# Level products of the chunked attention cut to their diagonal blocks and put in column groups of the array

## Chip, core and metric

The program runs on one core of one Trainium2 chip. The metric is the device time of one execution in microseconds, the median of three runs. TensorE (PE) has a matmul side and a weight-load side (PEld), VectorE is DVE, ScalarE is ACT, GpSimd is POOL, and SyncE (SP) issues nearly all transfers.

## What is computed

A two-layer trunk on 1024 latent and 128 context tokens of width 1024: a gated linear attention (GLA) layer, then a Fourier layer, each followed by a gated channel mixer. The change touches the GLA layer alone. For each of four heads (128 key channels, 256 value channels) and each of two scan directions:

```python
bcum = jnp.cumsum(gi, axis=2)
diff = bcum[:, :, :, None, :] - bcum[:, :, None, :, :]
decay = jnp.exp(jnp.where(lower[:, :, None], diff, -jnp.inf))
attn = jnp.einsum('bhik,bhjk,bhijk->bhij', qi, ki, decay)
o = (jnp.einsum('bhij,bhjv->bhiv', attn, vi)
     + jnp.einsum('bhik,bhkv->bhiv', qi * jnp.exp(bcum), state))
```

The weight of token j for token i has a decay that depends on the channel, so `attn` is no plain product of q and k.

## The kernel before

The kernel takes chunks of 128 tokens (nine of them: eight latent, one context), three to a column group `cg`, and does both directions at once. Within a chunk it builds the 128x128 matrix `A` (tile name `A`, keys on partitions, queries along columns) by levels. For a half block of s tokens in `LEVELS = (64, 32, 16, 8, 4, 2, 1)`, all pairs that lie in one block of 2s tokens but in different halves share a reference point, the boundary of the halves. The decay then splits into a factor on k and a factor on q: `e[:, 0]` and `e[:, 1]` (tile `le`) are made by a subtraction on POOL (line 535) and on DVE (537), one exponential on ACT (540), and a multiplication by k on POOL (541) and by q on DVE (546). The product of the two is taken for the whole 128x128 chunk, three chunks into one PSUM tile `lv` (line 549), and `copy_predicated` on DVE (551) takes from it, by a mask per level, what belongs to that level:

```python
for c in range(3):
    PE.matmul(ps[:, c * P:(c + 1) * P], lhsT=view(kk, kb + c * P, [1, P]),
              rhs=e[:, 1, c * P:(c + 1) * P], start=True, stop=True)
ins = V.copy_predicated(att.rearrange("p (c i) -> p c i", i=P), ...
```

The diagonal itself comes from an undecayed product of k and q (line 527), copied by ACT with a factor of 2 (528). So each cg has eight products of three matmuls, and there are twelve cg (four heads by three). All are fp32, and each fp32 matmul stands in the trace as two matmul records and two weight loads, here called passes. `A`, the states `sf` and `sb` and the values then make the output `o` (565 to 570), which is normed by way of `ov` (577) and multiplied by the gate `r`.

What surrounds it on PE: attention of head h is interleaved with the projections of head h+1 (`pr`, `pk`, `pq`, `pv`, lines 97 to 99, a product of three fp32r matmuls each), and head 3, which has no head after it, with its own `pr` and then with the first half of the output projection (`wo`). `mod_background` (line 175, tile `mods`) is a third strand: small products of 32 weight columns in four column groups of the array, given out by `tick` after every second level. The order on each engine is not written out by hand: the framework's scheduler lists the instructions by priority (`later(n)` moves a part back in it) as it simulates them, and each engine then runs its list in order. `le` has 4 buffers (tag `m3`, shared with `qb`), the PSUM tag of `lv`, `o`, `kt` and `kv` has 4, weight tiles `wr` have 2 and `wh` 6. The 14 buffers of tag `u` hold the normed input `Hp`, which the last `pr` product of head 3 reads; behind it they take the attention outputs `ot` that are read back, and the residual `x`.

Of the kernel before, what the change touches and what calls it, by code (L numbers as in the profile page):

```python
# [15 lines left out]
F32 = mybir.dt.float32  # L16
F32R = mybir.dt.float32r
I32 = mybir.dt.int32
U8 = mybir.dt.uint8
# [5 lines left out]
P = 128  # L25
# [5 lines left out]
CH = 384  # L31
# [14 lines left out]
def trunk(tc, a, o):  # L46
# [12 lines left out]
    def t15(name, dt=F32):  # L59
        return sb.tile([P, CH], dt, tag="t", bufs=5, name=name)  # L60

    def t30(name, dt=F32):
        return sb.tile([P, 2, CH], dt, tag="m3", bufs=4, name=name)
# [4 lines left out]
    def at_ps(name):  # L68
        return pp.tile([P, 512], F32, tag="at", bufs=4, name=name)
# [32 lines left out]
    def const(name, shape, dt=F32, src=None):  # L102
        t = con.tile(shape, dt, name=name)
        if src is not None:
            nc.sync.dma_start(t, src)
        return t
# [86 lines left out]
    def tick(n=1, behind=None):  # L193

        for _ in range(n):
            while queue:
                try:
                    with tc.issue_after(behind.ins) if behind else ExitStack():
                        next(queue[0])
                    break  # L200
                except StopIteration:
                    queue.pop(0)
# [177 lines left out]
    gng = const("gng", [P, 2], src=a["gng"])  # L380
    convw = const("convw", [P, 2, 3, NF], src=a["convw"])
    convb = const("convb", [P, 2, NF], src=a["convb"])
    mask = const("mask", [P, len(LEVELS), P], U8)
    mraw = sb.tile([P, 1032], F32, tag="wr", bufs=2, name="mraw")
    nc.sync.dma_start(mraw[:, :len(LEVELS) * P], a["mask"])
    V.tensor_copy(mask.rearrange("p l i -> p (l i)"), mraw[:, :len(LEVELS) * P])
    for ch in range(NCH):
        ev_glr(ch, pss[ch])

# [66 lines left out]
    def view(t, off, *dims):  # L456
        return bass.AP(tensor=t.tensor, offset=t.offset + off, ap=[list(t.ap[0]), *[list(d) for d in dims]])
# [21 lines left out]
    def kv(kt, v, c):  # L479
# [2 lines left out]
                  start=True, stop=True)  # L482
        return ps

    def attention(h, qk, pages):

        dec = sb.tile([P, 2, 9], F32, tag="dec", bufs=2, name="dec")
        for cg in range(3):
            S.activation(dec[:, :, 3 * cg:3 * cg + 3], view(pages[cg][:, BB], P - 1, [CH - P + 1, 2], [P, 3]),
                         AF.Exp, scale=1.0 / TAU)  # L490
        sf = page(f"sf{h}")
        nc.sync.dma_start(sf[:, :256], a["state"][0, h])
        for cg in range(3):
            v, bb = pages[cg][:, VV], pages[cg][:, BB]
            kt = khat(qk, bb, 0, cg)
            for c in range(3 * cg, 3 * cg + 3):
                if c == 7:
                    continue
                ps = kv(kt, v, c)
                if c == 8:  # L500
                    new_state(0, h, ps)
                else:
                    V.scalar_tensor_tensor(sf[:, (c + 1) * 256:(c + 2) * 256], sf[:, c * 256:(c + 1) * 256],
                                           dec[:, 0, c:c + 1], ps[:, :256], op0=ALU.mult, op1=ALU.add)
        yield
        s_b = sb.tile([P, 256], F32, tag="sb", bufs=4, name="sb")
        nc.sync.dma_start(s_b, a["state"][1, h])
        sbs = {7: s_b}
        for cg in (2, 1, 0):
            v, bb, r = pages[cg][:, VV], pages[cg][:, BB], pages[cg][:, RR]  # L510
            kt = khat(qk, bb, 1, cg)
            for c in range(3 * cg + 2, 3 * cg - 1, -1):
                if c == 0:
                    continue
                ps = kv(kt, v, c)
                if c == 8:
                    new_state(1, h, ps)
                else:
                    s_n = sb.tile([P, 256], F32, tag="sb", bufs=4, name="sb")
                    V.scalar_tensor_tensor(s_n, sbs[c], dec[:, 1, c:c + 1], ps[:, :256], op0=ALU.mult, op1=ALU.add)  # L520
                    sbs[c - 1] = s_n

            att = t15("A")
            ps = at_ps("lv")
            for c in range(3):
                s = cg * CH + c * P
                PE.matmul(ps[:, c * P:(c + 1) * P], lhsT=qk[:, s:s + P], rhs=qk[:, T + s:T + s + P], start=True, stop=True)
            S.activation(att, ps[:, :CH], AF.Copy, scale=2.0)
            for li, s in enumerate(LEVELS):
                nb = CH // (2 * s)  # L530
                base = cg * CH
                e = t30("le")
                ref = view(bb, s - 1, [2 * s, nb], [CH + 1, 2], [0, s])
                if s > 1:
                    G.tensor_tensor(view(e, 0, [2 * s, nb], [s, 2], [1, s]), ref,  # L535
                                    view(bb, 0, [2 * s, nb], [CH + s, 2], [1, s]), op=ALU.subtract)
                V.tensor_tensor(view(e, CH + s, [2 * s, nb], [-s, 2], [1, s]),
                                view(bb, s, [2 * s, nb], [CH - s, 2], [1, s]), ref, op=ALU.subtract)
                if s > 1:
                    S.activation(e, e, AF.Exp, scale=1.0 / TAU)  # L540
                    G.tensor_tensor(e[:, 0], e[:, 0], qk[:, base:base + CH], op=ALU.mult)  # L541
                    kk, kb = e, 0
                else:
                    S.activation(e[:, 1], e[:, 1], AF.Exp, scale=1.0 / TAU)
                    kk, kb = qk, base
                V.tensor_tensor(e[:, 1], e[:, 1], qk[:, T + base:T + base + CH], op=ALU.mult)
                ps = at_ps("lv")
                for c in range(3):
                    PE.matmul(ps[:, c * P:(c + 1) * P], lhsT=view(kk, kb + c * P, [1, P]),  # L549
                              rhs=e[:, 1, c * P:(c + 1) * P], start=True, stop=True)  # L550
                ins = V.copy_predicated(att.rearrange("p (c i) -> p c i", i=P),
                                  mask[:, li, None, :].to_broadcast([P, 3, P]),
                                  ps[:, :CH].rearrange("p (c i) -> p c i", i=P))
                if li % 2 == 0:
                    tick(1, behind=ins)
            qb = t30("qb")
            S.activation(qb, bb.rearrange("p (z i) -> p z i", z=2), AF.Exp, scale=1.0 / TAU)
            V.tensor_tensor(qb, qb, view(qk, T + cg * CH, [0, 2], [1, CH]), op=ALU.mult)

            po = [at_ps(f"o{d}") for d in range(2)]  # L560
            for d in range(2):
                for c in range(3):
                    cc = 3 * cg + c
                    out = po[d][:, c * P:(c + 1) * P]
                    PE.matmul(out, lhsT=v[:, c * 256 + d * P:c * 256 + (d + 1) * P], rhs=att[:, c * P:(c + 1) * P],
                              start=True, stop=(cc == 8))
                    if cc < 8:
                        PE.matmul(out, lhsT=sf[:, cc * 256 + d * P:cc * 256 + (d + 1) * P],
                                  rhs=qb[:, 0, c * P:(c + 1) * P], start=False, stop=False)
                        PE.matmul(out, lhsT=sbs[cc][:, d * P:(d + 1) * P],  # L570
                                  rhs=qb[:, 1, c * P:(c + 1) * P], start=False, stop=True)
            sq0, sq1 = t15("os0"), t15("os1")
            S.activation(sq0, po[0][:, :CH], AF.Square)
            S.activation(sq1, po[1][:, :CH], AF.Square)
            V.tensor_tensor(sq0, sq0, sq1, op=ALU.add)
            ps = at_ps("ov")
            PE.matmul(ps[:, :CH], lhsT=ones, rhs=sq0, start=True, stop=True)
            S.activation(sq1, ps[:, :CH], AF.Ln, bias=epsc[:, 0:1], scale=1.0 / 256.0)
            S.activation(sq1, sq1, AF.Exp, scale=-0.5)
            for d in range(2):  # L580
                o1 = t15("o1")
                V.scalar_tensor_tensor(o1, po[d][:, :CH], gng[:, d:d + 1], sq1, op0=ALU.mult, op1=ALU.mult)
                rv = r[:, d * CH:(d + 1) * CH]
                if h < 3:
                    V.tensor_tensor(rv, o1, rv, op=ALU.mult)
                else:
                    V.tensor_tensor(o1, o1, rv, op=ALU.mult)
                    split_ot(3, d, cg, o1)
            if h < 3:
                nc.sync.dma_start(ot_dram[h][:, :, cols(cg)].rearrange("d p t -> p d t"),  # L590
                                  r.rearrange("p (d t) -> p d t", d=2))
            yield
# [965 lines left out]
```

## Time and profile before

| what | value |
|---|---|
| median of 3 runs (lowest to highest) | 2561.12 us (2558.16 to 2563.42) |
| the profiled execution: time, span | 2564.86 us, 2563.0 us |
| PE, PEld busy in the span | 95%, 91% |
| DVE, ACT, POOL busy | 72%, 43%, 29% |
| mean granted TensorE clock | 0.981 of 2.4 GHz |
| mean DMA traffic | 121 GB/s |

Busy time of PE counts a matmul from its start to its modelled end, and matmuls overlap, so PE can look full while it moves little. Distances from start to start of matmuls say more. GLA attention lies between about 80 and 680 us. The profiled execution is 3.7 us above the median of the runs.

### The profile page before, as it was taken

Reading aid. Unit: us, or ns where it says so; the run is one execution under the profiler, and the core shown is the slowest. Engines: PE = TensorE matmul, PEld = TensorE weight load, DVE = VectorE, ACT = ScalarE, POOL = GpSimd, SP = SyncE. Lnnn points to the kernel's source line nnn. Section 1 sums busy time; section 2 is a strip of 40 time slices with the busy share of each in tenths; the row PEclk is TensorE's granted clock in tenths of the full one; section 3 lists DMA queues with packets and bytes.
Section 4 is the critical chain, followed back from the end, with each engine's and each line's share of the span. In section 5 each row is a group of like instructions: output and inputs, shape, how many; then the busy total and the mean of one; then the engine's idle time right before and its main releaser. Section 6 shows DMA issues by size and latency. Waiting matters only on the chain. (4 is left out here: it accounts for less than half of the span.)

```text
span 2563.0 us, 46543 instructions
## 1 busy us (share of the span) xinstructions
PE 2425.1 (95%) x18122; PEld 2329.2 (91%) x18122; DVE 1841.2 (72%) x3339; ACT 1089.3 (43%) x2086; POOL 730.9 (29%) x548
## 2 busy tenths in 40 slices
PE   5999999987999999999999998999899999999997
PEld 4998988877999999999999996998899999999997
DVE  7647475566699677777787877277987778778676
ACT  5435344445364323333345564344533333334553
POOL 3435454453202333444100005230144444410000
PEclk8999999998999999999999999999999999999999
DMA  7212222204233453232674357344223232267334
GB/s 263 69 54 89 80 80 82 67 21 146 87 116 124 132 172 104 91 96 83 212 248 135 112 153 216 107 156 144 90 87 117 83 96 87 80 229 224 93 86 125
DMA packets 200972, 309.85 MB, mean 121 GB/s; under 512 B 18288, under 2 KB 142064, under 8 KB 200752
## 3 DMA queue, kind: packets, MB, share of 16 engines
q1 hardware_dynamic: 196528, 302.66, 37.2%
q10 hardware_dynamic: 4224, 4.23, 0.5%
q8 instruction: 142, 2.33, 0.4%
q14 instruction: 78, 0.64, 0.1%
HBM read 233.71 MB, written 73.11 MB: 120 GB/s over the span
## 5 line engine op out<-in xcount | busy, mean ns | idle before, releaser
L98 PE MATMUL pd<-hl,wd 128*128 128x288 f32 x1112 | 328.7, 299 | 5.4 <-DVE hl L1085 5.2
L99 PE MATMUL pd<-hh,wd 128*128 128x288 f32 x1112 | 326.7, 297 | 0.0
L97 PE MATMUL pd<-hh,wd 128*128 128x288 f32 x1112 | 316.5, 298 | 5.5 <-ACT hh L1084 3.2
L809 POOL TENSOR_TENSOR s<-wa,s 128x512 fp32r<-128x512 f32 x114 | 157.0, 1377 | 278.6 <-ACT s L808 278.6
L1084 ACT ACTIVATE hh<-hr 128x288 fp32r<-128x288 f32 x308 | 133.2, 437 | 222.1 <-PE pd L98 213.3
L98 PEld LDWEIGHTS pd<-hl,wd 128*128 128x128 f32 x1112 | 210.8, 190 | 7.9 <-DVE hl L1085 7.4
L1085 DVE TENSOR_TENSOR hl<-hr,hh 128x288 fp32r<-128x288 f32 x308 | 138.5, 455 | 109.3 <-ACT hh L1084 108.7
L97 PEld LDWEIGHTS pd<-hh,wd 128*128 128x128 f32 x1112 | 204.2, 188 | 10.8 <-ACT hh L1084 5.7
L99 PEld LDWEIGHTS pd<-hh,wd 128*128 128x128 f32 x1112 | 210.4, 190 | 0.0
L809 POOL TENSOR_TENSOR a<-wa,a 128x512 fp32r<-128x512 f32 x76 | 100.1, 1318 | 334.7 <-ACT a L808 231.1
L808 ACT ACTIVATE s<-wa 128x512 fp32r<-128x512 f32 x120 | 75.5, 630 | 189.8 <-DVE wa L826 116.1
L977 ACT ACTIVATE hid<-hid 128x576 f32<-128x576 f32 x88 | 60.4, 686 | 161.5 <-DVE hid L972 102.0
L1074 DVE TENSOR_TENSOR wd<-wd,wd 128x512 fp32r<-128x512 f32 (+1 forms) x184 | 116.4, 642 | 9.7 <-ACT wd L1073 4.9
L808 ACT ACTIVATE a<-wa 128x512 fp32r<-128x512 f32 x80 | 50.3, 631 | 141.0 <-PE pa L99 76.2
L1073 ACT ACTIVATE wd<-wd 128x512 fp32r<-128x512 f32 (+1 forms) x184 | 104.4, 580 | 11.7 <-PE ps L99 4.0
L860 DVE TENSOR_TENSOR q<-q,ps 128x288 f32<-128x288 f32 x232 | 98.4, 444 | 10.1 <-PE ps L99 8.4
L535 POOL TENSOR_TENSOR le<-vbr 128x384 f32<-128x384 f32 x72 | 74.0, 1032 | 109.3 <-PE lv L549 95.5
L1208 POOL TENSOR_TENSOR fn<-fn 128x512 f32<-128x512 f32 x8 | 14.1, 1764 | 312.9 <-ACT wp L728 293.3
L541 POOL TENSOR_TENSOR le<-le,qk 128x384 f32<-128x384 f32 x72 | 91.6, 1278 | 35.6 <-ACT le L540 34.7
L97 PE MATMUL pa<-fh1x,a 128*128 128x288 f32 x320 | 95.3, 298 | 5.9 <-DVE c L860 3.6
L97 PE MATMUL ps<-fh1x,s 128*128 128x288 f32 x320 | 95.2, 298 | 3.0 <-DVE hid L917 3.0
L97 PE MATMUL ps<-fh0t,s 128*128 128x288 f32 x320 | 96.4, 302 | 1.4 <-DVE c L860 1.4
(689 smaller groups left out, 8852.5 us busy)
## 6 DMA issues: line engine op xcount, KB each, us to landing
hr<-hid SPq DMA_DIRECT2D x308, 144.0 KB, 2.2
wm<-in_wmod SPq DMA_DIRECT2D x112, 256.0 KB, 2.9
hid<-hid SPq DMA_DIRECT2D x44, 576.0 KB, 3.8
wa<-in_wup SPq DMA_DIRECT2D x40, 512.0 KB, 3.5
wg<-in_wup SPq DMA_DIRECT2D x40, 512.0 KB, 4.1
hid<-t SPq DMA_DIRECT2D x132, 144.0 KB, 3.3
wd<-in_wdn SPq DMA_DIRECT2D x16, 1024.0 KB, 8.0
wm<-in_wmod SPq DMA_DIRECT2D x96, 128.0 KB, 3.5
```

What stands on the lines that cost most here:

```text
L97: PE.matmul(ps, lhsT=wh, rhs=xh, start=first, stop=False, skip_group_check=skip)
L98: PE.matmul(ps, lhsT=wh, rhs=xl, start=False, stop=False, skip_group_check=skip)
L99: PE.matmul(ps, lhsT=wl, rhs=xh, start=False, stop=last, skip_group_check=skip)
L535: G.tensor_tensor(view(e, 0, [2 * s, nb], [s, 2], [1, s]), ref, view(bb, 0, [2 * s, nb], [CH + s, 2], [1, s]), op=ALU.subtract)
L541: G.tensor_tensor(e[:, 0], e[:, 0], qk[:, base:base + CH], op=ALU.mult)
L808: S.activation(w[name][:, :512], x, AF.Copy)
L809: (eng or G).tensor_tensor(w[name][:, 512:], x, w[name][:, :512].bitcast(F32), op=ALU.subtract)
L860: add.last = V.tensor_tensor(out[:, xs], x[:, xs], ps[s][:, :SUB], op=op)
L1073: S.activation(hi, x, AF.Copy)
L1074: low = V.tensor_tensor(lo, x, hi.bitcast(F32), op=ALU.subtract)
L1084: S.activation(hi[:, c], raw, AF.Copy)
L1085: V.tensor_tensor(lo[:, c], raw, hi[:, c].bitcast(F32), op=ALU.subtract)
```

## The change

Level s needs only the blocks of 2s tokens on the diagonal, so a product is now cut to them, but to no less than 32 columns: `n = max(2s, 32)`. The array is used in column groups: a matmul with `tile_position=(0, n*g)` takes n weight columns (keys) and n moving columns (queries), and writes to partitions n*g to n*g+n. The results of levels 16 to 1, and of the undecayed product, lie packed as 32 columns per chunk, in a new tile `near` of 96 columns; level 64 is unchanged on PE and is written to `A` first, by ACT, level 32 by a copy on ACT and one on DVE, and `near` is put into the four diagonal blocks of `A` at the end. The masks shrink to 32 columns. The files line up as 549 before, 492 after.

```diff
+    def diagonal(ps, n, kk, at, q):
+
+        for c in range(3):
+            for g in range(P // n):
+                PE.matmul(ps[n * g:n * g + n, c * n:(c + 1) * n], lhsT=view(kk, at + c * P + n * g, [1, n]),
+                          rhs=q[:, c * P + n * g:c * P + n * g + n], start=True, stop=True,
+                          **({} if n == P else dict(tile_position=(0, n * g))))
...
-    mask = const("mask", [P, len(LEVELS), P], U8)
+    mask = const("mask", [P, len(LEVELS) - 2, 32], U8)
...
-    V.tensor_copy(mask.rearrange("p l i -> p (l i)"), mraw[:, :len(LEVELS) * P])
+    for g in range(4):
+        b = slice(32 * g, 32 * g + 32)
+        V.tensor_copy(mask[b], mraw[b, 2 * P:len(LEVELS) * P].rearrange("p (l i) -> p l i", i=P)[:, :, b])
...
             ps = at_ps("lv")
-            for c in range(3):
-                s = cg * CH + c * P
-                PE.matmul(ps[:, c * P:(c + 1) * P], lhsT=qk[:, s:s + P], rhs=qk[:, T + s:T + s + P], start=True, stop=True)
-            S.activation(att, ps[:, :CH], AF.Copy, scale=2.0)
+            diagonal(ps, 32, qk, cg * CH, qk[:, T + cg * CH:T + (cg + 1) * CH])
+            S.activation(near, ps[:, :96], AF.Copy, scale=2.0)
...
-                for c in range(3):
-                    PE.matmul(ps[:, c * P:(c + 1) * P], lhsT=view(kk, kb + c * P, [1, P]),
-                              rhs=e[:, 1, c * P:(c + 1) * P], start=True, stop=True)
-                ins = V.copy_predicated(att.rearrange("p (c i) -> p c i", i=P),
-                                  mask[:, li, None, :].to_broadcast([P, 3, P]),
-                                  ps[:, :CH].rearrange("p (c i) -> p c i", i=P))
+                n = max(2 * s, 32)
+                diagonal(ps, n, kk, kb, e[:, 1])
+                if n == P:
+                    ins = S.activation(att, ps[:, :CH], AF.Copy)
+                elif n == 64:
+                    S.activation(att3[:64, :, :64], ps[:64, :192].rearrange("p (c i) -> p c i", i=64), AF.Copy)
+                    ins = V.tensor_copy(att3[64:, :, 64:], ps[64:, :192].rearrange("p (c i) -> p c i", i=64))
+                else:
+                    ins = V.copy_predicated(near.rearrange("p (c i) -> p c i", i=32),
+                                            mask[:, li - 2, None, :].to_broadcast([P, 3, 32]),
+                                            ps[:, :96].rearrange("p (c i) -> p c i", i=32))
...
+            for g in range(4):
+                b = slice(32 * g, 32 * g + 32)
+                src = near[b].rearrange("p (c i) -> p c i", i=32)
+                if g % 2:
+                    S.activation(att3[b, :, b], src, AF.Copy)
+                else:
+                    V.tensor_copy(att3[b, :, b], src)
```

A product so has 12 matmuls of 32 columns, or 6 of 64, where it had 3 of 128. As the scheduler sees other instructions, it also lays out another order of all engines through the whole of the GLA layer; behind it, from the Fourier layer's preparation on, the order is the same.

The first place is PE in head 0, its second cg (h=0, cg=1), where attention runs beside the `pv` projection of head 1. Before, from the undecayed product on:

```order
L527 MATMUL lv<-qk_686 128x128 x3
L549 MATMUL lv<-le 128x128 x4
L186 MATMUL mods_1554<-sel,mrow_1830 128x8
L549 MATMUL lv<-le 128x128 x5
L175 MATMUL mods_1856<-wm_1826,cs 32x128 x4
L175 MATMUL mods_1856<-wm_1828,cs 32x128 x4
L549 MATMUL lv<-le 128x128 x3
```

Now, in the same place:

```order
L492 MATMUL lv<-qk_689 32x32 x12
L492 MATMUL lv<-le 128x128 x3
L492 MATMUL lv<-le 64x64 x6
L492 MATMUL lv<-le 32x32 x9
L186 MATMUL mods_1580<-sel,mrow_1906 128x8
L492 MATMUL lv<-le 32x32 x15
L98 MATMUL pv_1793<-wv10l,h_303 128x256
L175 MATMUL mods_1945<-wm_1902,cs 32x128 x4
L175 MATMUL mods_1945<-wm_1904,cs 32x128 x4
L99 MATMUL pv_1793<-wv10h,h_303 128x256
L97 MATMUL pv_1793<-wv10h,h_304 128x256
```

The products still stand in blocks, but a stretch in column groups now starts and ends more often.

The second place is PE in head 3, its last cg (h=3, cg=0), where the only other work is the output projection `wo`. Before:

```order
L549 MATMUL lv<-le 128x128
L97 MATMUL wo_5503<-ot_5150,wo01h 128x384
L549 MATMUL lv<-le 128x128
L98 MATMUL wo_5503<-ot_5150,wo01h 128x384
L549 MATMUL lv<-le 128x128
L99 MATMUL wo_5503<-ot_5150,wo01l 128x384
```

Now:

```order
L492 MATMUL lv<-le 32x32
L98 MATMUL wo_6249<-ot_5720,wo03h 128x384
L492 MATMUL lv<-le 32x32
L99 MATMUL wo_6249<-ot_5720,wo03l 128x384
L492 MATMUL lv<-le 32x32
L97 MATMUL wo_6249<-ot_5723,wo03h 128x384
L492 MATMUL lv<-le 32x32
L98 MATMUL wo_6249<-ot_5723,wo03h 128x384
```

Before, single matmuls of a product alternated with `wo` too, three to a product, and both were of the full array; now it is twelve to a product in column groups, each between two full matmuls, and they have moved from `wo01` and `wo02` to the end of `wo02` and to `wo03`.

The third place is PE at the end of the same cg, where the last level is followed by `o` (588, 591, 593). Now:

```order
L492 MATMUL lv<-le,qk_4270 32x32
L99 MATMUL wo_6320<-ot_5723,wo03l 128x384
L492 MATMUL lv<-le,qk_4270 32x32 x9
L588 MATMUL o_6708<-A,vbr_5377 128x128
L591 MATMUL o_6708<-qb,sf_5652 128x128
L593 MATMUL o_6708<-qb,sb 128x128
```

Before, `o` of this cg alternated with `wo02`, and the whole of `wo03` (72 matmuls) stood behind it. Now all of the first half of `wo` stands in front, and behind the 18 matmuls of `o` come 18 of the second half that need no output of this cg. The cg before it (h=3, cg=1) changes in a similar way: its undecayed product alternates with `pr` one by one, and its other products stand in one block behind the last `pr`, where they alternated with `pr` before.

Counted over the whole program, PE goes from full matmuls into column groups and back 111 times before and 252 times now. 28 of the stretches are now a single `mods` product, of 2 before: in three places, beside `pr` of heads 0 to 2, eight of them that stood together alternate one by one with `pr`.

## Rows read from the trace of the kernel before

**Rows 1.** The page, busy time of the engines and the granted clock by 40 slices

```profile
PE 2425.1 (95%) x18122; PEld 2329.2 (91%) x18122; DVE 1841.2 (72%) x3339; ACT 1089.3 (43%) x2086; POOL 730.9 (29%) x548
...
PEclk8999999998999999999999999999999999999999
```

**Rows 2.** Stretches: us, busy PE, PEld, DVE, ACT, POOL; clock, DMA, GB/s

```profile
128.00:560.00 432.00, 407.26 (x3032) 371.39 (x3031) 253.34 (x403) 187.09 (x322) 196.64 (x153) 0.99 0.23 70
560.00:680.00 120.00, 102.08 (x599) 97.73 (x598) 74.87 (x116) 49.52 (x77) 43.02 (x29) 0.91 0.31 107
```

**Rows 3.** Waits, 80 to 660 us: in total, times, longest

```profile
POOL le L535 <- PE lv L549: 95.5, 46, 11.3
```

**Rows 4.** Tile lv: durations min/median/max in ns, first and last start

```profile
L549 PE MATMUL lv<-le x432: 270/275/378, 128.2 to 648.5; 128*128 128x128 f32 x144
L551 DVE COPY_PREDICATED A<-mask,lv x84: 572/584/608, 129.2 to 650.5; 128x384 f32<-128x384 uint8 x84
```

**Rows 5.** Order of time on PE, full, column, full: start, duration, passes

```profile
226.94 1.06 PE L549 MATMUL lv<-le 128*128 128x128 f32 x8
227.92 0.64 PE L175 MATMUL mods<-wm,cs 128*32 128x128 f32 x16
228.50 0.94 PE L549 MATMUL lv<-le 128*128 128x128 f32 x6
229.19 0.36 PE L97 MATMUL pv<-wv11h,h 128*128 128x256 f32 x1
```

**Rows 6.** Order of time on PE, column stretches between three fp32r matmuls

```profile
135.13 0.42 PE L175 MATMUL mods<-wm,cs 128*32 128x128 f32 x8
135.49 0.44 PE L99 MATMUL pr<-h,wr00l 128*128 128x384 f32 x1
135.77 0.34 PE L97 MATMUL pr<-h,wr00h 128*128 128x384 f32 x1
135.94 0.33 PE L98 MATMUL pr<-h,wr00h 128*128 128x384 f32 x1
136.21 0.43 PE L175 MATMUL mods<-wm,cs 128*32 128x128 f32 x8
```

**Rows 7.** Order of time on PE, a column stretch of two groups

```profile
1545.39 0.41 PE L175 MATMUL mods<-wm,cs 128*32 128x128 f32 x4
```

**Rows 8.** Between the cg of head 3: stretches, as rows 2

```profile
580.00:610.00 30.00, 16.15 (x96) 14.09 (x96) 22.99 (x37) 24.29 (x38) 12.39 (x10) 0.79 0.39 129
610.00:660.00 50.00, 49.61 (x301) 48.79 (x299) 27.51 (x46) 11.00 (x18) 13.57 (x9) 0.95 0.40 143
```

**Rows 9.** Order of time on PE there, in brackets what ended its wait

```profile
588.25 0.49 PE L565 MATMUL o<-A,vbr 128*128 128x128 f32 x2 [2.47 <-DVE A L551]
597.37 1.34 PE L577 MATMUL ov<-os,ones 128*128 128x384 f32 x2 [2.91 <-DVE os L575]
605.76 0.69 PE L97 MATMUL wo<-ot,wo00h 128*128 128x384 f32 x1 [7.05 <-ACT wo00h L86]
```

**Rows 10.** Tile le: durations min/median/max in ns

```profile
L535 POOL TENSOR_TENSOR le<-vbr x72: 826/916/1552, 81.5 to 640.2; 128x384 f32<-128x384 f32 x72
L540 ACT ACTIVATE le<-le x72: 827/844/850, 94.3 to 642.8; 128x768 f32<-128x768 f32 x72
L541 POOL TENSOR_TENSOR le<-le,qk x72: 1006/1316/1817, 98.5 to 643.8; 128x384 f32<-128x384 f32 x72
```

**Rows 11.** Order of time on ACT and PE after the last cg of head 3

```profile
658.48 0.47 ACT L574 ACTIVATE os<-o 128x384 f32<-128x384 f32 x1
661.57 0.89 PE L577 MATMUL ov<-os,ones 128*128 128x384 f32 x2 [1.96 <-DVE os L575]
665.35 0.95 ACT L601 ACTIVATE ot<-o 128x384 fp32r<-128x384 f32 x2
```

**Rows 12.** Stretches on PE: us, busy (instructions), granted clock, DMA, GB/s

```profile
1544.00:1548.00 4.00, 3.39 (x31) 1.00 0.99 328
...
1556.00:1560.00 4.00, 4.00 (x27) 0.60 0.95 278
```

More of the change, by code (lines that the diff above doesn't have):

```diff
@@ L523, in attention @@
             att = t15("A")
+            att3 = att.rearrange("p (c i) -> p c i", i=P)
+            near = sb.tile([P, 96], F32, tag="near", bufs=2, name="near")
             ps = at_ps("lv")
-            for c in range(3):
-                s = cg * CH + c * P
-                PE.matmul(ps[:, c * P:(c + 1) * P], lhsT=qk[:, s:s + P], rhs=qk[:, T + s:T + s + P], start=True, stop=True)
-            S.activation(att, ps[:, :CH], AF.Copy, scale=2.0)
+            diagonal(ps, 32, qk, cg * CH, qk[:, T + cg * CH:T + (cg + 1) * CH])
+            S.activation(near, ps[:, :96], AF.Copy, scale=2.0)
             for li, s in enumerate(LEVELS):
```

## The prediction

> **What bounds the kernel now.** I read the page first. PE is busy 95% of the span, at almost the full clock, and POOL only 29% [rows 1]. A mean over the program says little of one layer, so I cut the span into stretches next. In the attention of heads 0 to 2, PE is busy 407.26 of 432 us while DVE, ACT and POOL have much room [rows 2]. The waits agree: POOL, which begins each level, stands 95.5 us until PE has read a `le` buffer and frees it [rows 3]. So here PE sets the pace, and only PE time counts. The next look is at head 3, where PE loses 18 us in 120 [rows 2]: nearly 14 of them lie in 580 to 610, where it is busy 16.15 of 30, while the 50 us behind are packed, 49.61 busy [rows 8]. The single events name the cause: chains through `o` and `ov`, then weights `wo00h` that ACT rounds late [rows 9].
>
> **Prices on PE.** A product of three full fp32 matmuls is six passes; the trace has six from 228.50 to 229.19 [rows 5], so about 0.67 to 0.69 us a product at 0.112 a pass. The duration of one record, 0.275 [rows 4], is no price, since passes overlap.
>
> Twelve matmuls of 32 columns are 24 passes. If four column groups run at once, that is six rounds. The trace has such groups already, with 128 moving columns, in `mods`. Two runs of 8 passes start at 135.13 and at 136.21, with three fp32r matmuls of 384 between [rows 6]; such a matmul takes 0.17 when the next follows directly (135.77 to 135.94). So the run costs 1.08 - 3 x 0.17 = 0.57 us. Sixteen passes take 0.64 as recorded where eight take 0.42 [rows 5, 6], which is 0.22 for two rounds, 0.11 a round, what one full pass takes. Hence 0.57 = 2 x 0.11 + 0.35: about 0.34 us a run is the fixed price of going into column groups and back (PE empties, weights are loaded uncovered). Do groups run at once? A run of four passes (two groups) has 0.41, one of eight 0.42 or 0.43 [rows 6, 7]: yes.
>
> No row shows 32 moving columns. A round lies between a quarter of 0.11, 0.028, if it follows the columns, and 0.11, if it doesn't shrink. I take 0.028, since an fp32r matmul of 384 columns at 0.17 does follow its columns, and keep 0.11 as the other end. With it:
>
> - a block of 12 alone: 0.34 + 6 x 0.028 = 0.51, for 0.67
> - six of 64 columns alone: 0.34 + 6 x 0.055 = 0.67, no gain
> - a **single** 32-column matmul between two full ones: 0.34 + 2 x 0.028 = 0.40; twelve of these are 4.75 us, seven times what the product took
> - a change from 64 to 32 columns inside a stretch, estimated at 0.13 (one reload; bounds 0 to 0.34).
>
> So everything turns on how often PE changes modes, and this goes from 111 to 252.
>
> **The change part by part.**
>
> Heads 0 to 2, nine cg, products in blocks (the first place). Seven of eight products change, 7 x 0.67 = 4.7 us. Now: five more stretches, 1.7; six products of 32 columns, 36 rounds, 0.99; level 64's half blocks, 0.35; one reload 0.13: 3.17. That is -1.5 a cg, **-13.7** for nine. Against it, eight `mods` products that stood together alternate with `pr` in three places: seven or eight more stretches and their first rounds uncovered, 3.7 us each, **+11.1**; two further splits **+0.8**.
>
> Head 3, first cg (in blocks): **-1.9**. Second cg: twelve singles 4.75 and the rest in one block 2.36, against 8 x 0.67 = 5.4: **+1.7**. Last cg (the second place): 49 singles and a pair, 50 x 0.40 = 19.8; six single 64-column ones at 0.475, 2.85; blocks of 12 and 9, 1.0; the uncut product 0.67: 24.3 against 5.4, **+18.9**. It lies in the packed stretch [rows 8], so nothing covers it: POOL, ACT and POOL need 0.92, 0.84 and 1.32 for a level [rows 10], while PE now needs 12 x (0.40 + 0.17) = 6.8.
>
> The gap at 580 to 610. The last `pr` now stands ahead of the second cg's levels, and ACT and POOL round `wo00` ahead of that cg's `os`, so the 7.05 us wait [rows 9] should shrink. The last levels, which stood among `pr`, now stand behind it with nothing beside them; four `le` buffers cover all but about three levels, each 0.92 + 0.84 + 1.32 = 3.1 us from POOL to POOL, two of them overlapping: some 6 us of idle stay of 13.9. **-8**; bounds 0 and -13.9.
>
> The tail. From `os` at 658.48 through `ov` to `ot` ending at 666.3 is 7.8 us, with PE waiting 1.96 at `ov` [rows 11]; the rest was covered by `wo03`. Only 18 x 0.17 = 3.1 us of `wo` stand behind now: 7.8 - 3.1 - 1.96 = 2.7 uncovered, and some 1.3 for the copies of `near` into `A`, which are now the last step ahead of `o`: **+4**; bounds 0 and +8.
>
> Off PE. DVE's 60 `copy_predicated` on a quarter of the columns replace 84 of 0.584 [rows 4]; ACT gains some copies; the mask is cut in four copies, once. All of it lies beside PE, with DVE at 253 and ACT at 187 of 432 [rows 2]: 0. If PE were faster than POOL, whose half of a level (2.2 us) times 72 is 161 us, the cover would still hold. No DMA is moved past another that PE waits for.
>
> Sum: -13.7 + 11.1 + 0.8 - 1.9 + 1.7 + 18.9 - 8 + 4 = **+12.9 us**. That is against the profiled execution, 2564.86, which is 3.7 above the median of the runs; from the median, 2561.1 + 12.9 = **2574 us**.
>
> **The rivals.** All four are cases of this change at work; that it does not do what it says the order of PE excludes, since every product shows its 12 or 6 matmuls. A measurement of this kernel tells about 0.2% (5.1 us) from no change, so "same" is 2556 to 2566.2.
>
> A, the stretch is cheap: *faster*. Between fp32 matmuls the start of a 16-pass run to the next full one is 0.58 [rows 5], which is 4 x 0.11 + 0.14. If 0.14 is the whole fixed price, 252 - 111 = 141 more stretches cost 0.2 less each, -28: 2546. The point: at 0.285 the outcome becomes "same", under 0.21 "faster". Against it: the full run ahead lasts 0.98 for eight passes [rows 5], 0.08 too long, which makes 0.22 in all, and next to fp32r, where the singles stand, I read 0.35 [rows 6]. Faster 0.18.
>
> B, small rounds don't shrink: a round of 32 columns stays near 0.11. Then some 67 blocks x 6 x 0.08 = +32: 2606. Against it: nothing direct; for it, that nothing in the trace has so little to move. 0.13. The Trainium skill, "TensorE: Matmul & The Clock Gate", section "Wait — 56ns, not 53.3ns?", puts a floor of about 25 ns from start to start however few columns move; if column groups too waited for it, a block's 24 passes would take an estimated 0.6 us, some 0.43 more, and the 67 blocks 29 us more. The trace speaks against it: four further passes in other groups add 0.01 to 0.02 us, not 0.1 [rows 6, 7].
>
> C, the idle of head 3 absorbs the loss: the gap closes whole (-13.9) and the tail stays covered (0): 2574 - 5.9 - 4 = 2564, *same*. For it: the `wo` weights are ready earlier in the order. Against it: the last levels still run in a chain through POOL, ACT and DVE. With the part of A between 0.21 and 0.285: 0.20.
>
> D, the clock: the alternating stretch of the last cg keeps few columns busy for about 32 us. At 1544, busy 3.39 of 4 us, PE had the higher level (2.4 GHz, 1.00); from 1556 the mean is 0.60, so it stood at 1.2 GHz for most of those 4 us [rows 12]: the gate can fall within a program this busy. At half clock, some 20 us: 2594. 0.09.
>
> **How the numbers follow.** The forecast, 2574, keeps 0.40. Faster is A's 0.18; same is 0.20; the rest, 0.62, is slower (forecast, B, D). Slower holds most; its own range is 2567 to 2606. The range 2549 to 2604 leaves out A's end and about half of B.
>
> **What would show it.** Right: in heads 0 to 2 the GLA stretch ends within a few us of before; PE goes from `lv` to `wo` and back in 0.57 us a pair in head 3's last cg, and the gap before `wo` is smaller. Wrong: a block of 12 takes clearly under 0.4 or over 0.8 us; `wo` among the singles starts every 0.3 us; a new wait of PE for ACT's or DVE's copies into `A`; or a clock under 0.9 in the last cg.

## The result and the profile after

The change takes **2603.93 us** (2597.9 to 2606.28) against 2561.3 for the kernel before in the same comparison: a ratio of 1.0164, 95% interval 1.0143 to 1.0185, so 42.6 us slower. The forecast was 12.9 us slower: the sign was right, the size was not. The profiled execution has a span of 2603.6 us, 40.6 above that of before. Of the runs below, e9 had one disturbed execution of 5846.86 us, which is left out of its time and was the profiled one, so no waits are read from e9.

First the page after, for [rows 1]:

```profile
PE 2444.5 (94%) x19490; PEld 2312.8 (89%) x19490; DVE 1839.0 (71%) x3354; ACT 1096.7 (42%) x2130; POOL 735.3 (28%) x548
...
PEclk9999999998999999999999999999999999999999
```

The span is longer by 40.6 us and PE's share is nearly the same, 94% for 95%. Stretches show more, if both kernels are cut at the same point of the work: the first `o` of head 3 (its first cg) starts at 556 us before and at 573 after. Of the kernel after, columns as in [rows 2]:

```profile
80.00:573.00 493.00, 445.54 (x4475) 389.12 (x4473) 283.17 (x443) 211.41 (x394) 216.56 (x166) 0.98 0.22 67
573.00:720.00 147.00, 126.39 (x862) 105.38 (x863) 70.47 (x121) 48.33 (x82) 45.21 (x31) 0.93 0.26 86
```

And of the kernel before up to that point:

```profile
80.00:556.00 476.00, 448.49 (x3345) 410.13 (x3343) 278.17 (x435) 204.16 (x359) 215.31 (x165) 0.99 0.23 71
```

PE's busy time up to there fell by 2.95 us, and the forecast for the same work was -13.7 + 11.1 + 0.8 - 1.9 = -3.7. Yet the stretch is 17 us longer. So PE's work came out as priced, and the loss is idle time, which grew from 27.5 to 47.5 us. What PE waits for in 80 to 573 (total, times, longest), after:

```profile
PE lv L492 <- DVE le L557: 14.0, 15, 2.3
...
PE mods L175 <- DVE modT L187: 4.9, 7, 0.7
PE o L588 <- DVE A L578: 4.6, 8, 0.6
PE kv L484 <- ACT vbr L446: 3.4, 1, 3.4
```

and what it waited for there before, in 80 to 556:

```profile
...
PE lv L549 <- DVE le L546: 2.0, 5, 0.7
...
PE o L565 <- DVE A L551: 0.4, 1, 0.4
```

The wait for `le`, the factors that a product multiplies, went from 2.0 to 14.0 us, the one for `A` from 0.4 to 5.5 (4.6 and one of 0.9 for ACT's copies), and one for `modT`, 4.9, is new. Another new one, 3.4 us for `vbr`, is outweighed by smaller waits for `ke`, `qk` and a transfer (together 18.1 before, 12.0 after). POOL meanwhile waits as long in total for PE to free a buffer, before and after:

```profile
POOL le L535 <- PE lv L549: 77.2, 42, 10.0
POOL le L546 <- PE lv L492: 78.3, 27, 12.1
```

A level's steps did not keep their price either. DVE's subtraction (min/median/max in ns), before in 80 to 556 and after in 80 to 573:

```profile
L537 DVE TENSOR_TENSOR le<-vbr x72: 544/665/2745, 92.4 to 554.8; 128x384 f32<-128x384 f32 x72
...
L548 DVE TENSOR_TENSOR le<-vbr x73: 543/1046/2743, 90.5 to 573.0; 128x384 f32<-128x384 f32 x73
```

In total it took 70.4 us for 52.8, while DVE's multiplication stayed at 64.9 for 63.6.

The prices on PE, in the order of time on PE after. Singles among `wo`, in the last cg of head 3:

```profile
671.03 0.45 PE L99 MATMUL wo<-ot,wo03l 128*128 128x384 f32 x1
671.41 0.25 PE L492 MATMUL lv<-le 128*32 128x32 f32 x2
671.59 0.45 PE L97 MATMUL wo<-ot,wo03h 128*128 128x384 f32 x1
671.97 0.25 PE L492 MATMUL lv<-le 128*32 128x32 f32 x2
```

A pair takes 671.97 - 671.41 = 0.56 us; 0.57 was forecast. The gap at 580 to 610 of before, [rows 9], looks so now:

```profile
602.20 1.89 PE L492 MATMUL lv<-le 128*128 128x128 f32 x66
611.34 0.55 PE L492 MATMUL lv<-le 128*32 128x32 f32 x24 [7.25 <-DVE le L557]
612.62 0.55 PE L492 MATMUL lv<-le 128*32 128x32 f32 x24 [0.73 <-DVE le L557]
613.72 0.55 PE L492 MATMUL lv<-le,qk 128*32 128x32 f32 x24 [0.55 <-DVE le L557]
618.04 0.77 PE L588 MATMUL o<-A,vbr 128*128 128x128 f32 x2 [3.77 <-DVE A L578]
618.60 0.63 PE L591 MATMUL o<-qb,sf 128*128 128x128 f32 x2
619.03 0.63 PE L593 MATMUL o<-qb,sb 128*128 128x128 f32 x2
```

Four levels are ready and go at once, in 1.89 us; then PE has nothing to do for 12.3 us in four waits. And what follows is slow too: two `o` matmuls start 0.43 us apart, twice the two passes of 0.112 of a full matmul. Three stretches of 2 us there, columns as in [rows 2]:

```profile
606.00:608.00 2.00, 0.00 (x0) 0.00 (x0) 2.00 (x6) 2.00 (x7) 0.00 (x0) 1.00 0.00 0
...
618.00:620.00 2.00, 1.96 (x9) 1.99 (x10) 2.00 (x3) 1.95 (x3) 1.37 (x2) 0.50 0.95 387
...
622.00:624.00 2.00, 1.62 (x11) 1.31 (x11) 0.60 (x1) 1.86 (x3) 2.00 (x2) 1.00 0.00 0
```

When `o` begins, the granted clock is half. That is not new: before, the mean over 580 to 610 was 0.79 [rows 8].

### The profile page after: what moved, and what is told of

Read it like the earlier page. It is cut to its first block, busy times and chain, and to the rows that moved or that the text cites. A ratio compares the mean times of both kernels' runs of the same rounds, so it can differ in the third digit from the quotient of the medians.

```text
span 2603.6 us, 49371 instructions
## 1 busy us (share of the span) xinstructions
PE 2444.5 (94%) x19490; PEld 2312.8 (89%) x19490; DVE 1839.0 (71%) x3354; ACT 1096.7 (42%) x2130; POOL 735.3 (28%) x548
## 5 line engine op out<-in xcount | busy, mean ns | idle before, releaser
L883 DVE TENSOR_TENSOR c<-q,pa 128x288 f32<-128x288 f32 x80 | 36.1, 451 | 87.0 <-PE pa L99 85.2
```

The costliest lines, as they stand in the source:

```text
L883: add.last = V.tensor_tensor(out[:, xs], x[:, xs], ps[s][:, :SUB], op=op)
```

## The experiments

The scheduler lays a new order for every kernel, so a plain edit changes two things. Most runs therefore hold PE's list: every PE matmul up to the end of attention is tied, in issue order only, behind the one that stands ahead of it in a given list. It costs no instruction. The other engines' lists are still laid out by the scheduler around it. The core of it:

```diff
+    for x, y in zip(seq, seq[1:]):
+        tc.add_manual_dep(y, x.name, mybir.DependencyInfo(mybir.DependencyClass.NoSync, mybir.DependencyReason.DATA),
+                          reason="order")
```

| run | time, us | ratio to before (95%) |
|---|---|---|
| the change | 2603.93 | 1.0164 (1.0143 to 1.0185) |
| e1, the change on PE's order of before | 2602.99 | 1.0166 (1.0149 to 1.0184) |
| e2, full products on PE's order of the change | 2609.93 | 1.0199 (1.0180 to 1.0218) |
| e3, as e1, products in one block | 2600.41 | 1.0160 (1.0142 to 1.0177) |
| e4, the change, products in one block | 2575.26 | 1.0064 (1.0047 to 1.0082) |
| e5, as e4, `mods` in blocks too | 2562.82 | 1.0008 (0.9995 to 1.0021) |
| e6, as e4, copies into `A` on DVE | 2595.36 | 1.0138 (1.0119 to 1.0158) |
| e7, packed levels first | 2584.97 | 1.0093 (1.0071 to 1.0115) |
| e8, as e7, in blocks | 2564.80 | 1.0002 (0.9989 to 1.0015) |
| e9, as e5, k factor on DVE | 2549.80 | 0.9957 (0.9943 to 0.9972) |
| e10, as e9, own order | 2543.57 | 0.9933 (0.9918 to 0.9948) |
| e11, as e5, three `le` buffers | 2640.29 | 1.0311 (1.0294 to 1.0329) |
| e12, before, three `le` buffers | 2644.50 | 1.0327 (1.0309 to 1.0345) |
| e13, before, k factor on DVE | 2556.86 | 0.9982 (0.9966 to 0.9998) |
| e14, the change, k factor on DVE | 2575.43 | 1.0045 (1.0029 to 1.0061) |
| e15, as e10, packed levels first | 2540.11 | 0.9911 (0.9883 to 0.9940) |

### Order or products: e1 to e4

Theory 1: the order that the change brings, and its waits, cost the time. Theory 2: the small products and the copies around `near` and `A` do, wherever they stand. e1 puts the four (level 32: two) small matmuls in the place of each full one:

```diff
-seq: PE's matmuls in the order laid out for the change
+seq: the order of before; for full matmul (product p, chunk c) the small ones of (p, c)
```

> The change with TensorE's list held to the order of before: each of the three full matmuls of a product is replaced, in its place, by its four (level 32: two) small ones; the other engines' lists are laid out around it. PE enters column groups 176 times, before 111, the change 252. Theory 1 (the order, and the waits it makes, cost the time; the small products are as cheap as forecast): 12 x (4.7 - 0.99 - 0.35) = -40 for the products, 65 x 0.34 = +22 for the stretches, +1 for reloads: about 2544, and PE waits for le in heads 0 to 2 as little as before (2 us). Theory 2 (the small products and the copies around near and A cost the time, wherever they stand): 2575 to 2600. In between, both.

2602.99: theory 1 alone falls. The waits of PE in e1, 80 to 594 us:

```profile
PE o L625 <- DVE A L615: 24.9, 9, 3.8
PE lv L529 <- DVE le L594: 12.9, 12, 2.8
```

The list of before puts `o` right behind the last product, because then one `copy_predicated` finished `A`. Now four copies more stand between. One such place, POOL, DVE, ACT and PE in order of time:

```profile
239.82 1.16 POOL L589 TENSOR_TENSOR le<-le,qk 128x384 f32<-128x384 f32 x1 [2.18 <-ACT le L588]
240.21 1.19 DVE L594 TENSOR_TENSOR le<-le,qk 128x384 f32<-128x384 f32 x1
...
240.97 0.40 PE L529 MATMUL lv<-le,qk 128*32 128x32 f32 x24
241.33 1.19 DVE L585 TENSOR_TENSOR le<-vbr 128x384 f32<-128x384 f32 x1
...
243.51 0.56 DVE L594 TENSOR_TENSOR le<-le,qk 128x384 f32<-128x384 f32 x1 [0.99 <-ACT le L588]
243.55 1.37 POOL L589 TENSOR_TENSOR le<-le,qk 128x384 f32<-128x384 f32 x1 [1.45 <-ACT le L588]
243.99 0.26 DVE L604 COPY_PREDICATED near<-mask,lv 128x96 f32<-128x96 uint8 x1
244.15 1.19 DVE L585 TENSOR_TENSOR le<-vbr 128x384 f32<-128x384 f32 x1
244.28 0.57 ACT L613 ACTIVATE A<-near 32x96 f32<-32x96 f32 x2 [0.80 <-DVE near L604]
...
245.26 0.49 DVE L615 COPY A<-near 32x96 f32<-32x96 f32 x2
```

The last product starts at 240.97 and `A` is whole at 245.75. Of these 4.8 us the copies take 0.57 and 0.49. In most of the rest `copy_predicated` and then DVE's copies stand on DVE behind two subtractions and a multiplication of the next cg, and behind 0.99 us in which that multiplication waits for ACT.

> The reverse: the kernel before, its full products and its masks, with TensorE's list held to the order of the change; a full matmul stands where the last small one of its chunk stood. 133 stretches, all of mods. Theory 1: the alternating mods products +11, the emptied gap of head 3 and waits for le in heads 0 to 2 some +15: 2580 to 2590, with PE waiting for le 10 us or more. Theory 2: the mods alone, about 2570, and waits for le as before.

2609.93. The wait for `le` in 80 to 594 is 25.1 us, which theory 1 allowed (10 or more); the time is 20 us above its range. So e2 is worse than both theories: a list laid out for other products fits badly, whichever way round.

> As the first, but all 12 (or 6) small matmuls of a product stand together, at the place of the third full matmul of before: 143 stretches. Both theories agree on the difference to the first run if a stretch costs 0.34: 33 fewer, -11. Theory 1: about 2533. If a stretch cost half of that, -5.

2600.41, 2.6 us below e1: some 8 us of the saving on the stretches was lost, 3.4 of it in a longer wait at `o` (28.3 for 24.9). With a list that does not fit, e3 does not price a stretch. e4 does, on the change's own list:

```diff
-seq: the order laid out for the change
+seq: the same, but all matmuls of a product at the place of its last one
```

> The change on its own order, but all matmuls of a product stand together, at the place of the last: the singles among wo and pr of head 3 are gone, 190 stretches in place of 252. 62 x 0.34 = 21 us less than the change: 2583, if singles in head 3 cost what I forecast and lie on the path; if the waits in head 3 take their place, within 8 us of the change.

2575.26: 28.7 us less than the change for 62 stretches fewer, 0.46 each where I had 0.34; the singles of head 3 cost more than the stretch by itself, and why is not settled. The wait for `le` in heads 0 to 2 is the same, 13.9 us, and so is the lag when head 3 begins (+15.3 us on before for +17.0). The singles and the wait are two separate costs.

### Stretches and the copies: e5 to e8

> As e4_new_order_blocks (2575), and the eight mods matmuls of two k also stand together, at the place of the last: 152 stretches in place of 190, and no single mods. At 0.34 a stretch 38 fewer give -13: about 2562, no longer slower than before. If PE waits for le and A take the place of it: 2570 or more.

2562.82, as forecast: 38 stretches fewer gave 12.4 us, 0.33 each (0.38 by the ratios). The block of 12 among `wo` can be read in e5's order of time on PE:

```profile
656.65 0.34 PE L135 MATMUL wo<-ot,wo03l 128*128 128x384 f32 x1
656.91 0.40 PE L528 MATMUL lv<-le 128*32 128x32 f32 x24
657.24 0.45 PE L133 MATMUL wo<-ot,wo03h 128*128 128x384 f32 x1
657.53 0.34 PE L134 MATMUL wo<-ot,wo03h 128*128 128x384 f32 x1
```

657.53 - 656.65 = 0.88 for the block and two `wo` of 0.17: the block is 0.54, forecast 0.51. But e5, with PE's saving paid out, is only as fast as before. PE was busy 431.25 us of 480 up to the first `o` of head 3 (80 to 560), 17 less than before, and waits:

```profile
PE lv L528 <- DVE le L593: 15.3, 20, 2.3
...
PE o L624 <- ACT A L612: 6.7, 7, 1.0
```

e6 asks whether ACT's new copies make `le` late:

```diff
-                    ins = S.activation(att, ps[:, :CH], AF.Copy)
+                    ins = V.tensor_copy(att, ps[:, :CH])
...
-                    S.activation(att3[:64, :, :64], ps[:64, :192].rearrange("p (c i) -> p c i", i=64), AF.Copy)
+                    V.tensor_copy(att3[:64, :, :64], ps[:64, :192].rearrange("p (c i) -> p c i", i=64))
```

> As e4_new_order_blocks, same list on PE, but the copies of levels 64 and 32 into A are all DVE's, none of ACT's. Theory: these copies, which wait for PE, stand on ACT ahead of the exponentials of later levels, and so make PE wait for le (13.9 us in heads 0 to 2). If so that wait falls below 6 us and the time by about 8: 2567. If the level chain is late for another reason (POOL, DVE, four buffers), the wait stays at 12 or more and the time within 4 us of 2575 or above it, since DVE has two more copies a cg.

2595.36, 20 us slower than e4: the theory falls. The wait for `le` grew from 13.9 to 26.0 us (80 to 592), so work added to DVE hurts; what ends this wait is DVE's multiplication.

e7 takes the other levels first, puts `near` into `A`, then copies only the off-diagonal blocks of levels 32 and 64:

```diff
+ORDERED = (16, 8, 4, 2, 1, 32, 64)
...
-            for li, s in enumerate(LEVELS):
+            for li, s in enumerate(ORDERED):
...
+                    S.activation(att3[:64, :, 64:], p3[:64, :, 64:], AF.Copy)
+                    ins = V.tensor_copy(att3[64:, :, :64], p3[64:, :, :64])
```

> The change with another order of the levels: 16, 8, 4, 2, 1 first, then the packed results go into A, then levels 32 and 64 are copied into A by their off-diagonal blocks only. The scheduler lays out its own order; 202 stretches, 57 singles in head 3 and 26 single mods. If the step from near to A behind the last level is what PE waits for at o (5.5 us in heads 0 to 2, 6.1 in head 3), this wait falls to under 2 us, and with 50 fewer stretches (-17) the time is about 2578. If that step is not the cause, the stretches alone: 2587.

2584.97, between its two numbers. The wait at `o` did not fall: 6.8 us in 80 to 564, after 5.5. The step from `near` to `A` is not by itself what makes `o` late.

> As e7_packed_first, with all matmuls of a product together and the mods in groups of eight: 119 stretches (before 111). By my prices: products -40, 8 stretches more +3, and the new waits for le some +12 with what stays of the gap in head 3: about 2545, faster than before. If the waits for le grow as the products shrink, 2560 or more.

2564.80: no faster than e5 with 33 stretches fewer. Its waits in 80 to 562:

```profile
PE lv L529 <- DVE le L594: 18.5, 23, 1.7
...
PE lv L529 <- POOL le L589: 6.0, 6, 1.7
```

24.5 us for `le` now. What PE saves comes back as a wait for the chain that makes a level.

### The chain that makes a level: e9 to e12

New theory: the chain POOL, ACT, POOL and DVE cannot deliver levels faster than the full products used them. e9 shortens POOL's part, with PE's list of e5:

```diff
-                    G.tensor_tensor(e[:, 0], e[:, 0], qk[:, base:base + CH], op=ALU.mult)
+                    V.tensor_tensor(e[:, 0], e[:, 0], qk[:, base:base + CH], op=ALU.mult)
```

> As e5_blocks_and_mods (2563; PE waits 15.3 us for le in heads 0 to 2), same list on PE, but the multiplication of le by k is DVE's, not POOL's. POOL's part of a level goes from about 2.4 us (1.15 + 1.31) to 1.15. Theory: the chain that makes a level is late for the shorter products, and POOL is its slowest part; then the wait falls by half or more, and the time to about 2553. If DVE is the slowest part (its two steps take 1.05 and 1.19 beside POOL), its third step makes the wait longer: 2570 or more.

2549.80: 13.0 us faster than e5, as the theory has it for the time. Whether the wait fell as well is read in e10.

> As e9_multiply_on_dve, but the list on PE is the one that the scheduler lays for this division of the work, again with products and mods together. If e9 fails only because its lists don't fit each other, this is 5 us or more faster than e9; if not, within 4.

2543.57: 6.2 us faster again, and 0.67% faster than before. Waits in 80 to 546:

```profile
PE o L624 <- ACT A L612: 10.1, 8, 1.5
...
PE lv L528 <- DVE le L593: 4.2, 9, 0.9
```

From 15.3 to 4.2 us for `le`. Why DVE can bear a third step shows in the durations (min/median/max in ns) of the tile `le`. In e5:

```profile
L593 DVE TENSOR_TENSOR le<-le,qk x73: 544/1191/1373, 97.8 to 562.2; 128x384 f32<-128x384 f32 x73
...
L588 POOL TENSOR_TENSOR le<-le,qk x63: 994/1310/1463, 97.5 to 561.8; 128x384 f32<-128x384 f32 x63
```

In e10:

```profile
L593 DVE TENSOR_TENSOR le<-le,qk x74: 545/551/1029, 98.0 to 552.2; 128x384 f32<-128x384 f32 x74
...
L588 DVE TENSOR_TENSOR le<-le,qk x64: 543/554/560, 97.5 to 551.7; 128x384 f32<-128x384 f32 x64
```

In e5 DVE's multiplication took 1191 ns in the median, mostly behind an instruction of POOL that had begun before it (last section); in e10 both multiplications on DVE together take 551 + 554 = 1105. POOL's help cost DVE more than it took off it. The move shortens POOL's part and takes these collisions away at once; no run separates the two.

e11 and e12 try the loop through the buffers (`bufs=4` to `bufs=3` for tag `m3`):

> As e5_blocks_and_mods with three buffers of le in place of four. Theory: in the changed kernel POOL can start a level only when a product has read a buffer, and PE then waits for it: with one buffer fewer the wait for le grows by 15 us or more, the time to 2580 or more. If the wait is not one for the loop through the buffers, 2565.

> The kernel before, its own order held on PE, with three buffers of le in place of four. With full products PE is the slower side, and one buffer fewer costs less than in e11: under 10 us by theory (2570 or less). If it costs as much as in e11, the loop through the buffers was as near to the path before the change as behind it.

2640.29 and 2644.50. The layers behind use this tag as well, so the totals say little. Up to the first `o` of head 3 the two kernels lag 25.5 us (e11) and 31.2 us (e12) behind the kernel before. PE's wait for the factors, in 80 to 582 of e11

```profile
PE lv L528 <- DVE le L593: 29.8, 9, 4.2
```

and in 80 to 588 of e12:

```profile
PE lv L586 <- POOL le L578: 26.7, 12, 3.2
```

Against its own kernel with four buffers, e11 begins head 3 21.9 us later (e5 lags 3.6) and e12 31.2. So one buffer fewer costs the old kernel at least as much. My expectation that only the changed kernel stands at the edge of this loop is wrong: three buffers were too few before, too.

### The control: e13 to e15

> The kernel before, with the multiplication of le by k on DVE in place of POOL, and the order that the scheduler lays for that. Theory: before, PE is the limit in heads 0 to 2 (it waits 2 us for le), so a shorter chain gives nothing: 2556 to 2566, and the 17 us of e10 are what the small products save. Rival: the gain of e9 and e10 is the shorter chain's alone, and small products give nothing: 2545 to 2550.

2556.86 (ratio 0.9982, 0.9966 to 0.9998): a small gain. With e5 and e10 this makes four corners:

| k factor on | full products | small products in blocks |
|---|---|---|
| POOL | 2561 | 2563 (e5) |
| DVE | 2557 (e13) | 2544 (e10) |

Small products give nothing while the chain is slow, and 0.0049 of the time, 12.5 us, when it is not (0.9982 - 0.9933). The rival, that the shorter chain alone explains e10, falls: the chain alone gives 0.0018. (The kernels with blocks also hold PE's list, the other two don't.)

> The change with the multiplication on DVE and nothing else: own order, singles among wo and pr of head 3 and of mods (235 and 17 stretches, as the change). Theory: the shorter chain gives what it gave in e9 (12 us) and the singles still cost 28 + 12: about 2590.

2575.43, 28.5 us less than the change, twice what I expected. The singles are all still there; the wait for `le` fell from 14.0 to 3.9 us (80 to 552), for `modT` and `A` from 10.4 to 2.3, and head 3 begins 4.3 us ahead of before, where the change was 17.0 behind. The same move puts e13 3.9 us ahead there, so with the faster chain the change is level with the old kernel up to there (-0.4, forecast -3.7). In head 3 e14 then loses 19.6 us.

> As e10 (2544) with the levels in the order of e7, so that the packed results go into A before the last two levels: the wait of PE for A at o, 11.3 us in heads 0 to 2 in e10, should fall by half: 2538. If the last two levels, now products of 64 and 128 columns with their own copies, end as late as the packed ones did, within 4 us of 2544.

2540.11, the fastest measured; its interval overlaps that of e10. The wait for `A` at `o` fell as said, to 2.6 us in 80 to 535, but the one for `le` rose to 15.0. What bounds e15 is open.

## Why the prediction came out as it did

- **What bounds the kernel.** Right that PE sets the pace before; PE waited only 2.0 us for `le` then. Wrong to read POOL's 95.5 us of waiting [rows 3] as room: POOL waits as long after the change, 78.3 us for 77.2, while PE waits for the chain. e12 shows that the loop through four buffers had less than one buffer to spare, and e6 that two more copies a cg on DVE cost the changed kernel 20 us.
- **Prices on PE.** Held. A single among `wo` 0.56 with its neighbour (0.57 forecast), a block 0.54 (0.51), a stretch 0.33 to 0.38 (0.34) in e5; only e4's singles gave back more, 0.46. The small moving operand is cheap, and the column groups run at once: rivals A and B are out. The floor on starts that the Trainium skill states ("TensorE: Matmul & The Clock Gate", "Wait — 56ns, not 53.3ns?") doesn't add up over column groups: a block's 24 passes take 0.33 us from their start to the next `wo` (656.91 to 657.24), 14 ns each.
- **Heads 0 to 2 and head 3's first cg.** Forecast -3.7 for PE's work, measured -2.95 in busy time, but +17.0 in the end. **This is the step that failed: "All of it lies beside PE", priced at 0, and "the cover would still hold".** I had checked the cover with one engine's mean throughput, POOL's 161 us in 432 (and that counts the 72 levels of all four heads against the time of three). What PE meets is a chain through three engines, each with a list in which two cg stand mixed. The rows had a hint that I did not use: `le` cost POOL 0.92 and 1.32 us [rows 10], and DVE's steps beside them were not read at all. The missing term is +20.7 us; the waits for `le`, `A` and `modT` grew by 12.0 + 5.1 + 4.9 = 22.0, less what other waits lost. e14 shows the cause: with the k factor on DVE the same products, in an order of their own, begin head 3 21.3 us earlier, where the same move gives the old kernel 3.9 (e13); with PE's list held it gives e5 13.0 in all (e9). DVE's subtraction became longer besides (the result section): such longer steps go with POOL's (last section), and how much of the missing term they are is open.
- **The gap in head 3.** Forecast some 6 us of idle time left, measured 12.3. This is the term that was mis-sized, and the trace suggests the same cause: the fifth level of that cg began only when PE had read a buffer, and PE waited 7.25 us for it and not 3.1, since copies of `ot` stand ahead of its steps on ACT and DVE. No run changes this by itself. So -8 was about -1.6.
- **Last cg and tail.** From the first `o` of head 3 to the end the change lost 23.6 us more, where my terms make 1.7 + 18.9 - 8 + 4 = 16.6; with the gap's 6.3 added it is 22.9. Split into work and idle time, from 556 to 900 before and from 573 to 940.6 after, PE's busy time grew by 21.1 us (my 1.7 + 18.9 = 20.6) and its idle time by 2.5 (my -8 + 4 = -4). e4 confirms that singles are the largest part.
- **Rival C** (the idle of head 3 absorbs the loss) was wrong for the same reason. **Rival D** (the clock) is out for the last cg: singles ran at full pace (0.56 a pair). Half clock stood in the gap, as before, and the mean granted clock hardly moved: 0.99 to 0.98 up to the first `o` of head 3, 0.94 to 0.93 from there to 720.

Sum: 12.9 + 20.7 + 6.3 = 39.9, against 40.6 between the two profiled executions. The 20.7 is itself measured less forecast, so this sum only shows that nothing large is left over in head 3.

## What to carry to other kernels

When the engine that sets the pace gets less work, price the chain that feeds it as a latency, buffer by buffer and list by list, not by the busy share or the waiting time of its engines: here POOL waited 78 us for PE, and PE 14 for the chain that POOL begins. Small matmuls in column groups pay only in blocks, since each way in and out cost 0.33 to 0.46 us here, and a list scheduler that sees every small matmul as separate will scatter them; holding the list for PE alone gave 28.7 and 12.4 us. Change the feeding chain together with the products: either alone was worth 5 us or less, both 17.

## What was not expected of the hardware

- **POOL and DVE slow each other, and which one began first decides who waits.** In the rows of e1 above, DVE's multiplication (line 594) that begins 0.39 us after POOL's takes 1.19 us and ends 0.42 us after it. The one that begins 0.04 us ahead of POOL's takes 0.56 us, and POOL's then takes 1.37, where its shortest in e5 is 0.99. In the whole trace of e5, 64 of DVE's 84 multiplications found a POOL instruction running and ended 0.41 to 0.42 us after its end; the 20 others took 0.54 to 0.56 us. The Trainium skill, "SBUF — State Buffer", section "SBUF: two separate sides", has the two share one pair of ports as an exclusive lock, which a DVE instruction with two SBUF inputs also needs; these rows agree with that.
- **The clock can be low when a wait ends.** After the wait at `o` two `o` matmuls start 0.43 us apart, from 618.60 on. PE stood idle in 606 to 608, still at 1.00 (2.4 GHz); in 618 to 620 it is busy 1.96 of 2 us at 0.50 (1.2 GHz), and from 622 on it has 1.00 again.
